# More pairs with seven products, and operand sums kept in DRAM, in the down projections of a two-layer decoder trunk

## The chip, the core and the metric

The kernel runs on one core of one Trainium2 chip. The metric is device time in microseconds (us). The engines are named as the profile names them: PE (TensorE, matrix products; PEld is its weight loads), DVE (VectorE), ACT (ScalarE), POOL (GpSimd) and SP (SyncE). Each engine executes its own instructions in the order in which the build has put them, and waits on semaphores for the others. Here SP does nothing but issue DMAs, and POOL little else.

## The reference

The model has two layers over 256 tokens of width 2048, all in float32: a gated linear attention layer and a block-sparse attention layer, each followed by the same channel mixer. The change lies in the two channel mixers (a convolutional SwiGLU with 5632 hidden features):

```python
def conv_ffn(x, norm_w, w_up, conv_w, conv_b, w_down):
    S = x.shape[1]
    h = rms_norm(x, norm_w) @ w_up
    hp = jnp.pad(h, ((0, 0), (CONV_WIDTH - 1, 0), (0, 0)))
    acc = conv_b
    for j in range(CONV_WIDTH):
        acc = acc + conv_w[j] * hp[:, j:j + S]
    a, u = jnp.split(acc, 2, axis=-1)
    return (jax.nn.silu(a) * u) @ w_down
```

```python
    for layer in range(DEPTH):
        if layer < N_A_LAYERS:
            h = h + gla_mixer(...)
        else:
            ...
            h = h + moba_mixer(...)
        h = h + conv_ffn(h, ffn_norm[layer], ffn_w_up[layer], ffn_conv_w[layer],
                         ffn_conv_b[layer], ffn_w_down[layer])
    return h
```

## The kernel before

**Products and their parts.** Every operand of a matrix product is kept as a high part (a cast to fp32r) and a low part (the remainder), and a product is high times high, low times high and high times low. `split` (L371) does this for activations; for weights ACT makes `whi` (L127) and DVE makes `wlo` (L128).

**The weight stream.** `WeightStream` brings all weights in chunks of 128 x 2048 floats (1 MB), in the order in which they are used, on SP's queue. A chunk lands in one of four `raw` buffers (`wraw`), and each half of 1024 columns is split into a `whi` and a `wlo`: three halves out of four into one of three `parts` buffers, the fourth into two slots of the pool `big`. `step` hands out one half; `prefetch` keeps the splits two to three halves ahead and the loads four chunks ahead (six in the down projections). A buffer of `raw` is free again when the second `wlo` made from it is done. `big` has 35 slots of 4 KB a partition, which also hold hidden activations, sums and residuals.

**Up projections.** There are 44 groups in each layer, two steps for one half of them each: `gemm` (L325) does 16 matmuls of 512 columns with `whi` (L332) and 16 of 256 with `wlo` (L334) in two steps. Then `ffn` (L634) makes the hidden activations (`hid`, 22 tiles, one for each pair of k-tiles below). During these stages `make_ahead` (L301) also prepares weight sums for the down projections: it loads a chunk of `w_dn` into a `raw` buffer (L308), adds in place with four DVE operations (L306, L307), and stores 1 MB to DRAM (`tsum`, L311, POOL's queue). The jobs are due at fixed counts of steps: the first after 24 and then every 12 for layer 0, the first after 8 and then every 12 for layer 1.

**Down projections.** `down` (L664) computes the 2048 output features in two blocks of 1024. A block goes over 22 pairs of k-tiles in an order that `ORDERS` writes out. An ordinary pair is a 2 x 2 block product with eight products of three matmuls each (L694). A pair with a `+` or `^` uses the seven products of the Strassen-Winograd scheme: 21 matmuls, with four sums of the activations and four sums of the weights. The weight sums come back from `tsum`, for `+` into a `raw` buffer and for `^` into two slots (`sums`). The sums of the activations (`combine`, L605, tile names `comb` and `whole`) are made in the up projections for the pairs in `EARLY`, and otherwise in the down projections by `combine_parts` (L629), at places 1, 3, 5, ... of a block. Of every four pairs with sums, three get a slot of their own, and the fourth uses what the three leave free. After the last pair with seven products, `u_sums` (L729) adds the products up; the last up to three ordinary pairs of a block (`_tail`) then run in two halves, and each half is closed with further additions (L776 for the last layer). The next block needs the PSUM banks that these additions free.

The order of instructions on each engine is decided by the framework's scheduler on a timeline of its own; the semaphores between engines follow from the tiles.

Of the kernel before, what the change touches and what calls it, by code (L numbers as in the profile page):

```python
# [18 lines left out]
S = 256  # L19
# [18 lines left out]
def _order(text):  # L38


    return [(int(k.rstrip("+^")), k[len(k.rstrip("+^")):]) for k in text.split()]


EARLY = (1, 3, 5, 7)
ORDERS = [[_order("0 1+ 2 3^ 4 5+ 6 7^ 8 9+ 11^ 10 13+ 15^ 12 16+ 17^ 14 19+ 18 20 21"),
           _order("0 2 4 6 1+ 3^ 8 5+ 7^ 10 9+ 11^ 12 13+ 15^ 14 16+ 17^ 18 19+ 20 21")],
          [_order("0 1+ 2 3^ 4 5+ 6 7^ 8 9+ 11^ 10 13+ 15^ 12 16+ 17^ 14 19+ 18 20 21"),
           _order("0 1+ 2 3+ 5^ 4 7+ 9^ 6 11+ 13^ 8 15^ 16+ 10 17^ 19^ 18 12^ 14^ 20 21")]]


def _tail(order):
# [89 lines left out]
def trunk(ctx: ExitStack, tc: tile.TileContext, xT, cst, msk, w1p, w2a, w_k, w_qa, w_v2, w_v, w_g, w_go,  # L141
# [2 lines left out]
    V, A, T = nc.vector, nc.scalar, nc.tensor  # L144

    keep = ctx.enter_context(tc.tile_pool(name="keep", bufs=1))
    big = ctx.enter_context(tc.tile_pool(name="big", bufs=35))
    raw = ctx.enter_context(tc.tile_pool(name="raw", bufs=4))
    parts = ctx.enter_context(tc.tile_pool(name="parts", bufs=3))
    tmp = ctx.enter_context(tc.tile_pool(name="tmp", bufs=6))  # L150
# [5 lines left out]
    def slot(shape, dt, name):  # L156
        return big.tile(shape, dt, name=name, tag="slot")
# [143 lines left out]
    def make_ahead(layer, w, first, every):  # L301

        def work(at):
            t = raw.tile([128, 2048], F32, name="wraw")
            b12, b11, b22, b21 = (t[:, 512 * i:512 * i + 512] for i in range(4))
            jobs = [lambda: V.tensor_sub(b22, b22, b12), lambda: V.tensor_sub(b12, b12, b11),  # L306
                    lambda: V.tensor_add(b11, b22, b11), lambda: V.tensor_sub(b21, b21, b11)]  # L307
            nc.sync.dma_start(t, ws.rows(w, at[0], 2048 * at[1]))  # L308
            for i, job in enumerate(jobs):
                after(4 + i, job)  # L310
            after(8, lambda: nc.gpsimd.dma_start(parked[layer][at], t))  # L311

        for i, at in enumerate(ahead[layer]):
            after(first + every * i, lambda at=at: work(at))
# [56 lines left out]
    def split(dst_hi, dst_lo, src):  # L371
        A.copy(dst_hi, src)
        V.tensor_sub(dst_lo, src, dst_hi.bitcast(F32))
# [19 lines left out]
                self.col = column_rstd(self.acc)  # L393


    make_ahead(0, w_dn0, 24, 12)
    nrm = Norm(C_GN, "xw", columns=True)
    for p in range(2):
        nrm.operand(p)
# [202 lines left out]
        for n in norms:  # L602
            after(2, n.close)

    def combine(k, hid_k, halves_):  # L605

        (a0, a1), (b0, b1) = halves_
        t = temp("comb", (128, 4, 128))
        V.tensor_add(t[:, 0], a1, b1)
        V.tensor_sub(t[:, 1], t[:, 0], a0)  # L610
        V.tensor_sub(t[:, 2], a0, a1)
        V.tensor_sub(t[:, 3], b0, t[:, 1])
        n = len(combos)
        if n % 4 < 3:
            rooms.append(slot([128, 4, 2, 128], F32R, "comb"))
            c = rooms[-1]
            split(c[:, 0:3, 0], c[:, 0:3, 1], t[:, 0:3])
            combos[k] = [(c[:, f, 0], c[:, f, 1]) for f in range(3)]
        else:
            combos[k] = [(c[:, 3, 0], c[:, 3, 1]) for c in rooms[-3:]]  # L620
            for f, parts_ in enumerate(combos[k]):
                split(*parts_, t[:, f])
        combos[k].append((hid_k[:, 0, 128:S], hid_k[:, 0, S + 128:]))
        split(*combos[k][3], t[:, 3])

    rooms = []
    combos = {}

    def combine_parts(k, hid):  # L629
        t = temp("whole")  # L630
        V.tensor_add(t, hid[k][:, :, :S], hid[k][:, :, S:])
        combine(k, hid[k], [(t[:, i, :128], t[:, i, 128:]) for i in range(2)])

    def ffn(layer, nrm, then):  # L634
        xs = rows(nrm.xs)
        hid = []
        combos.clear()
        whole = [None, None]
        cw = C_CW + layer * 3 * 2 * FT
        cb = C_CB + layer * 2 * FT  # L640
        for j in range(FT):
            ps = gemm(xs, KT)
            t = both(ps, "up")
            V.tensor_mul(t, t, bc(nrm.rstd))  # L644
            au = temp("au")
            for i in range(2):
                n = i * FT + j
                A.activation(au[:, i, :], t[:, i, :], AF.Identity, bias=col(cb + n),  # L648
                             scale=col(cw + 2 * 2 * FT + n))
                V.scalar_tensor_tensor(au[:, i, 1:], t[:, i, :S - 1], col(cw + 2 * FT + n), au[:, i, 1:],  # L650
                                       op0=OP.mult, op1=OP.add)
                V.scalar_tensor_tensor(au[:, i, 2:], t[:, i, :S - 2], col(cw + n), au[:, i, 2:],  # L652
                                       op0=OP.mult, op1=OP.add)
            A.activation(au[:, 0, :], au[:, 0, :], AF.Silu)
            V.tensor_mul(au[:, 0, :], au[:, 0, :], au[:, 1, :])
            if j % 2 == 0:
                hid.append(slot([128, 2, 2 * S], F32R, "hid"))
            split(hid[-1][:, j % 2, :S], hid[-1][:, j % 2, S:], au[:, 0, :])
            whole[j % 2] = (au[:, 0, :128], au[:, 0, 128:])
            if j % 2 and j // 2 in EARLY:  # L660
                combine(j // 2, hid[-1], whole)
        then(hid)

    def down(layer, hid, ready, jobs):  # L664

        def late(k):
            return lambda: combine_parts(k, hid)

        done = set(EARLY)
        for b, order in enumerate(ORDERS[layer]):  # L670
            new = [k for k, seven in order if seven and k not in done]
            done |= set(new)
            todo = dict(jobs.get(b, {}))
            for i, k in enumerate(new):
                todo.setdefault(1 + 2 * i, []).append(late(k))
            low = acc_ps.tile([128, 2, 512], F32, name="acc")
            p = {2: low[:, 0], 3: low[:, 1], 4: bank("p4", (128, 512)), 8: bank("p8", (128, 512))}
            left = dict.fromkeys(range(1, 9), 0)
            for k, seven in order:
                for n in ((1, 5, 7, 6, 4, 3, 2) if seven else (2, 3, 4, 8, 2, 3, 4, 8)):  # L680
                    left[n] += 3
            begun = set()

            def prods(*todo):

                w = step()
                for n, _, _ in todo:
                    if n not in p:
                        two = acc_ps.tile([128, 2, 512], F32, name="acc")
                        p.update({n: two[:, 0], {1: 6, 5: 7}[n]: two[:, 1]})  # L690
                for xi, wi in ((0, 0), (1, 0), (0, 1)):
                    for n, x, f in todo:
                        left[n] -= 1
                        T.matmul(p[n], x[xi], w[wi][:, 512 * f:512 * f + 512], start=n not in begun, stop=left[n] == 0)  # L694
                        begun.add(n)

            def part(k, i, t):
                x = hid[k][:, i, 128 * t:]
                return x[:, :128], x[:, S:S + 128]

            def comb(k, f):
                return combos[k][f]

            last = max(i for i, (k, seven) in enumerate(order) if seven)
            tail = [k for k, _ in order[len(order) - _tail(order):]]
            for i, (k, seven) in enumerate(order[:len(order) - len(tail)]):
                for job in todo.get(i, ()):
                    job()
                if seven:
                    prods((1, part(k, 0, 0), 0))  # L710
                    prods((3, comb(k, 3), 0), (2, part(k, 1, 0), 1))
                    prods((6, comb(k, 1), 1), (5, comb(k, 0), 0))
                    prods((7, comb(k, 2), 0), (4, part(k, 1, 1), 1))
                else:
                    for a in range(2):
                        prods(*((n, part(k, a, t), f)
                                for n, t, f in ((2, 0, a), (3, 0, 1 - a), (4, 1, a), (8, 1, 1 - a))))
                if i == last:
                    sums = ready(b, p)
            for f, (n0, n1) in enumerate(((2, 4), (3, 8))):  # L720
                for i, k in enumerate(tail):
                    for job in todo.get((f, i), ()):
                        job()
                    prods(*((n, part(k, a, t), a) for a in range(2) for n, t in ((n0, 0), (n1, 1))))
                if f:
                    ws.prefetch(cur[0])
                sums(f, (n0, n1))
# [217 lines left out]
        ox.append(o)  # L945

    xkv = []
    make_ahead(1, w_dn1, 8, 12)
    after(12, bias_rows)
    for p in range(NP):  # L950
        after(26 + p, lambda p=p: xkv.append(make_xw(p, C_KVN, "xkv")))
# [148 lines left out]
```

## Time and profile before

| | us |
|---|---|
| median of 3 runs (2212.78 to 2212.98) | 2212.93 |
| the profiled execution | 2212.01 |
| its span | 2210.2 |
| DVE busy | 1731.5 |
| ACT busy | 1292.6 |
| up projections of layer 0, some | 412 to 877 |
| its down blocks | 877 to 989, 989 to 1105 |
| up projections of layer 1, some | 1505 to 1982 |
| its down blocks | 1983 to 2095, 2095 to 2206 |

The stages in the lower rows are times from the start of the span. In the profile's rows, `out<-in` names the tile written and the tiles read, without buffer numbers; `xN` counts instructions; after the bar stand the busy time, the mean time of one in ns, and the idle time of the engine just before them with what ended it. `SPq` and `POOLq` are the queues on which SP and POOL issue DMAs; the figure at the end of such a row is the median time from issue to landing. In the windows each engine has its busy time and, in brackets, its instructions; then come the granted clock of PE as a share of full speed, the mean share of the 16 DMA engines, and GB/s.

### The profile page before, as it was taken

How to read it: one execution, taken by the hardware profiler on the slowest of the kernel's cores; microseconds unless marked ns; L12 is line 12 of the kernel's file. 1: busy time of each engine (PE TensorE's matmuls, PEld its weight loads, DVE VectorE, ACT ScalarE, POOL GpSimd, SP SyncE). 2: the span in 40 equal slices, each digit the busy share in tenths (PEclk: the TensorE clock that was granted, in tenths of full speed). 3: DMA queues.
4: the chain of work that ended last, by engine and by line, in shares of the span. 5: the costliest groups of instructions: out<-in, count | busy, mean ns of one | idle time of the engine just before them, and what ended most of it. 6: DMA issues, size and time to landing. Idle time of an engine off the chain costs nothing.

```text
span 2210.2 us, 30840 instructions
## 1 busy us (share of the span) xinstructions
PE 2203.1 (100%) x11742; PEld 1902.4 (86%) x11742; DVE 1731.5 (78%) x2478; ACT 1292.6 (58%) x1825; POOL 69.5 (3%) x107
## 2 busy tenths in 40 slices
PE   9999999999999999999999999999999999999999
PEld 7889888888888888888888888888888888888887
DVE  6676877788888887977777676678888888788876
ACT  6655644665555555656556665546665555556564
POOL 0000000000000000000010000000000000000000
PEclk9999999999999999999999999999999999999999
DMA  7675577676677775788867665676777676768895
GB/s 299 214 253 201 208 271 270 244 272 249 240 265 247 248 266 201 277 288 293 303 213 265 246 243 195 218 265 251 259 265 248 247 266 234 261 238 293 285 364 192
DMA packets 86631, 561.20 MB, mean 254 GB/s; under 512 B 10145, under 2 KB 10673, under 8 KB 27602
## 3 DMA queue, kind: packets, MB, share of 16 engines
q1 hardware_dynamic: 76050, 499.85, 63.8%
q0 software_dynamic: 9856, 58.80, 6.8%
q8 instruction: 92, 1.51, 0.3%
q10 hardware_dynamic: 576, 0.58, 0.1%
q14 instruction: 57, 0.47, 0.1%
HBM read 504.64 MB, written 54.55 MB: 253 GB/s over the span
## 4 chain that ended last, share of the span: by engine, by line
PE 98%; DMA 1%; DVE 1%; ACT 0%; issue 0%; SPq 0%; ACTq 0%; DVEq 0%
PE acc L332 40%; PE acc L334 21%; PE acc L694 13%; PE acc L347 10%; PE p L694 6%; PE acc L350 5%; PE sT L538 0%; DVE wlo L128 0%; DMA wraw<-w_v 0%; PE tr L891 0%; ACT whi L127 0%; PE s L909 0%; DMA wraw<-w_dn 0%; PE pT L929 0%; PE z L444 0%; PE oT L424 0%
## 5 line engine op out<-in xcount | busy, mean ns | idle before, releaser
L127 ACT CAST whi<-wraw 128x1024 fp32r<-128x1024 f32 (+1 forms) x832 | 839.5, 1024 | 604.9 <-PE acc L332 319.1
L128 DVE TENSOR_TENSOR wlo<-wraw,whi 128x1024 fp32r<-128x1024 f32 (+1 forms) x832 | 973.0, 1188 | 273.7 <-ACT whi L127 155.3
L332 PE MATMUL acc<-xw,whi 128*128 128x512 f32 x3328 | 796.9, 391 | 0.0
L332 PEld LDWEIGHTS acc<-xw,whi 128*128 128x128 f32 x3328 | 610.8, 188 | 117.9
L334 PEld LDWEIGHTS acc<-xw,wlo 128*128 128x128 f32 x3328 | 426.8, 191 | 16.1
L334 PE MATMUL acc<-xw,wlo 128*128 128x256 f32 x3328 | 432.6, 283 | 0.0
L694 PE MATMUL acc<-whi,hid 128*128 128x512 f32 x612 | 183.5, 390 | 0.0
L694 PE MATMUL p<-whi,hid 128*128 128x512 f32 x428 | 139.4, 389 | 0.0
L694 PEld LDWEIGHTS acc<-whi,hid 128*128 128x128 f32 x612 | 114.6, 188 | 23.6
L347 PE MATMUL acc<-whi,xkv 128*128 128x512 f32 x512 | 134.5, 394 | 0.0
L347 PE MATMUL acc<-whi,xw 128*128 128x512 f32 x512 | 129.0, 392 | 1.6 <-ACT whi L127 1.6
L650 DVE SCALAR_TENSOR_TENSOR au<-up,cs,au 128x255 f32<-128x255 f32 x176 | 83.0, 481 | 48.0 <-ACT au L648 47.7
L347 PEld LDWEIGHTS acc<-whi,xw 128*128 128x128 f32 x512 | 95.3, 188 | 22.5 <-ACT whi L127 2.5
L347 PEld LDWEIGHTS acc<-whi,xkv 128*128 128x128 f32 x512 | 93.7, 188 | 17.8
L360 ACT COPY up<-acc 128x512 f32<-128x512 f32 x88 | 51.5, 585 | 88.9 <-PE acc L334 88.8
L694 PE MATMUL acc<-wlo,hid 128*128 128x512 f32 x306 | 100.1, 390 | 0.3 <-DVE wlo L128 0.3
L648 ACT ACTIVATE au<-up,cs 128x256 f32<-128x256 f32 x176 | 96.1, 593 | 6.5 <-DVE up L644 5.8
L694 PEld LDWEIGHTS p<-whi,hid 128*128 128x128 f32 x428 | 80.3, 188 | 16.8
L694 PE MATMUL acc<-whi,comb 128*128 128x512 f32 x276 | 83.0, 389 | 0.0
L652 DVE SCALAR_TENSOR_TENSOR au<-up,cs,au 128x254 f32<-128x254 f32 x176 | 80.9, 476 | 0.0
L694 PE MATMUL p<-wlo,hid 128*128 128x512 f32 x214 | 70.9, 389 | 0.0
L350 PE MATMUL acc<-wlo,xkv 128*128 128x512 f32 x256 | 69.8, 391 | 0.0
(261 smaller groups left out, 2076.7 us busy)
## 6 DMA issues: line engine op xcount, KB each, us to landing
wraw<-w_up SPq DMA_DIRECT2D x176, 1024.0 KB, 6.1
wraw<-w_dn SPq DMA_DIRECT2D x88, 1024.0 KB, 4.9
tsum<-wraw POOLq DMA_DIRECT2D x46, 1024.0 KB, 6.4
wraw<-w_dn SPq DMA_DIRECT2D x46, 768.0 KB, 5.9
wraw<-tsum SPq DMA_DIRECT2D x23, 1024.0 KB, 6.6
sums<-tsum SPq DMA_DIRECT2D x46, 512.0 KB, 6.9
wraw<-w_g SPq DMA_DIRECT2D x16, 1024.0 KB, 5.5
wraw<-w_go SPq DMA_DIRECT2D x16, 1024.0 KB, 5.2
```

The source lines that it names most:

```text
L127: nc.scalar.copy(hi[:, a:b], src[:, a:b])
L128: nc.vector.tensor_sub(lo[:, a:b], src[:, a:b], hi[:, a:b].bitcast(F32))
L332: T.matmul(ps[:, b, :], two[i][0][:, c:c + 128], xs(kt), start=kt == 0, stop=False)
L334: T.matmul(ps[:, b, :S], two[i][1][:, c:c + 128], xs(kt)[:, :S], start=False, stop=kt == kts - 1)
L347: T.matmul(ps[:, t, :], xs(kt)[:, x0 + 128 * t:x0 + 128 * t + 128], hi[:, c:c + 512], start=kt == 0 and x0 == 0, stop=False)
L350: T.matmul(ps[:, t, :], xs(kt)[:, 128 * t:128 * t + 128], lo[:, c:c + 512], start=False, stop=kt == KT - 1)
L360: A.copy(t, ps[:, :, S:])
L648: A.activation(au[:, i, :], t[:, i, :], AF.Identity, bias=col(cb + n), scale=col(cw + 2 * 2 * FT + n))
L650: V.scalar_tensor_tensor(au[:, i, 1:], t[:, i, :S - 1], col(cw + 2 * FT + n), au[:, i, 1:], op0=OP.mult, op1=OP.add)
L652: V.scalar_tensor_tensor(au[:, i, 2:], t[:, i, :S - 2], col(cw + n), au[:, i, 2:], op0=OP.mult, op1=OP.add)
L694: T.matmul(p[n], x[xi], w[wi][:, 512 * f:512 * f + 512], start=n not in begun, stop=left[n] == 0)
```

## The change

The number of pairs with seven products goes from 46 to 53: 11 to 13 in the first block of each layer, 11 to 12 in the second block of layer 0, and 13 to 15 in the second block of layer 1. The orders change with it; the halved tail of the first blocks is two pairs instead of three. For the pairs in `ASIDE` the four activation sums are made in the up projections, three of them split into a slot and written to DRAM (`aside`, 384 KB, POOL's queue), and brought back into their room by a DMA on POOL's queue in the first block of the down projections, where they were made before. The sums still made late in a first block are those of pairs 17, 19, 12 and 14; the sums of 10 and 8 are made in the last block of layer 1. The jobs of a block now stand at its places 0, 1, 2, ... instead of 1, 3, 5, .... A pair that the last block doesn't use as a seven (`kept` False) has its fourth sum in its room and not in `hid`. `make_ahead` prepares 25 chunks instead of 22 for layer 0 (every 11 steps instead of 12) and 28 instead of 24 for layer 1 (from step 6 every 10 instead of from step 8 every 12). `big` gets a 36th slot, and the buffer for software DMA descriptors is halved.

```diff
--- before.py
+++ after.py
@@ -41,11 +41,13 @@
     return [(int(k.rstrip("+^")), k[len(k.rstrip("+^")):]) for k in text.split()]
 
 
+
 EARLY = (1, 3, 5, 7)
-ORDERS = [[_order("0 1+ 2 3^ 4 5+ 6 7^ 8 9+ 11^ 10 13+ 15^ 12 16+ 17^ 14 19+ 18 20 21"),
-           _order("0 2 4 6 1+ 3^ 8 5+ 7^ 10 9+ 11^ 12 13+ 15^ 14 16+ 17^ 18 19+ 20 21")],
-          [_order("0 1+ 2 3^ 4 5+ 6 7^ 8 9+ 11^ 10 13+ 15^ 12 16+ 17^ 14 19+ 18 20 21"),
-           _order("0 1+ 2 3+ 5^ 4 7+ 9^ 6 11+ 13^ 8 15^ 16+ 10 17^ 19^ 18 12^ 14^ 20 21")]]
+ASIDE = (9, 11, 13, 15, 16)
+MADE = (9, 11, 13, 17, 15, 16, 19, 12, 14, 10, 8)
+FIRST = "0 1+ 2 3^ 5+ 4 7^ 9+ 6 11^ 13+ 8 15^ 16+ 10 17^ 19+ 18 12^ 14+ 20 21"
+ORDERS = [[_order(FIRST), _order("0 2 4 6 1+ 3^ 8 5+ 7^ 10 9+ 11^ 18 13+ 15^ 14 16+ 17^ 19+ 12^ 20 21")],
+          [_order(FIRST), _order("0 1+ 3^ 2 5+ 7^ 9+ 4 11^ 13+ 15^ 6 16+ 17^ 19+ 18 12^ 14^ 10^ 8^ 20 21")]]
 
 
 def _tail(order):
@@ -144,7 +146,7 @@
     V, A, T = nc.vector, nc.scalar, nc.tensor
 
     keep = ctx.enter_context(tc.tile_pool(name="keep", bufs=1))
-    big = ctx.enter_context(tc.tile_pool(name="big", bufs=35))
+    big = ctx.enter_context(tc.tile_pool(name="big", bufs=36))
     raw = ctx.enter_context(tc.tile_pool(name="raw", bufs=4))
     parts = ctx.enter_context(tc.tile_pool(name="parts", bufs=3))
     tmp = ctx.enter_context(tc.tile_pool(name="tmp", bufs=6))
@@ -393,7 +395,7 @@
                 self.col = column_rstd(self.acc)
 
 
-    make_ahead(0, w_dn0, 24, 12)
+    make_ahead(0, w_dn0, 24, 11)
     nrm = Norm(C_GN, "xw", columns=True)
     for p in range(2):
         nrm.operand(p)
@@ -602,34 +604,60 @@
         for n in norms:
             after(2, n.close)
 
-    def combine(k, hid_k, halves_):
-
+    combos = {}
+    rooms = []
+    aside = dram.tile([2, len(ASIDE), 128, 768], F32R, name="aside")
+
+    def room(k, hid_k, kept):
+
+
+        n = len(combos)
+        if n % 4 < 3:
+            rooms.append(slot([128, 4, 2, 128], F32R, "comb"))
+            combos[k] = [(rooms[-1][:, f, 0], rooms[-1][:, f, 1]) for f in range(3)]
+        else:
+            combos[k] = [(c[:, 3, 0], c[:, 3, 1]) for c in rooms[-3:]]
+        combos[k].append((hid_k[:, 0, 128:S], hid_k[:, 0, S + 128:]) if kept else
+                         (rooms[-1][:, 3, 0], rooms[-1][:, 3, 1]))
+        return rooms[-1] if n % 4 < 3 else None
+
+    def sums(halves_):
         (a0, a1), (b0, b1) = halves_
         t = temp("comb", (128, 4, 128))
         V.tensor_add(t[:, 0], a1, b1)
         V.tensor_sub(t[:, 1], t[:, 0], a0)
         V.tensor_sub(t[:, 2], a0, a1)
         V.tensor_sub(t[:, 3], b0, t[:, 1])
-        n = len(combos)
-        if n % 4 < 3:
-            rooms.append(slot([128, 4, 2, 128], F32R, "comb"))
-            c = rooms[-1]
-            split(c[:, 0:3, 0], c[:, 0:3, 1], t[:, 0:3])
-            combos[k] = [(c[:, f, 0], c[:, f, 1]) for f in range(3)]
+        return t
+
+    def combine(k, hid_k, halves_, kept=True):
+
+        t = sums(halves_)
+        own = room(k, hid_k, kept)
+        if own is not None and not kept:
+            return split(own[:, :, 0], own[:, :, 1], t)
+        if own is not None:
+            split(own[:, 0:3, 0], own[:, 0:3, 1], t[:, 0:3])
         else:
-            combos[k] = [(c[:, 3, 0], c[:, 3, 1]) for c in rooms[-3:]]
-            for f, parts_ in enumerate(combos[k]):
-                split(*parts_, t[:, f])
-        combos[k].append((hid_k[:, 0, 128:S], hid_k[:, 0, S + 128:]))
+            for f in range(3):
+                split(*combos[k][f], t[:, f])
         split(*combos[k][3], t[:, 3])
 
-    rooms = []
-    combos = {}
-
-    def combine_parts(k, hid):
+    def put_aside(layer, k, hid_k, halves_):
+        t = sums(halves_)
+        c = slot([128, 3, 2, 128], F32R, "aside")
+        split(c[:, :, 0], c[:, :, 1], t[:, 0:3])
+        nc.gpsimd.dma_start(aside[layer, ASIDE.index(k)], c.rearrange("a b c d -> a (b c d)"))
+        split(hid_k[:, 0, 128:S], hid_k[:, 0, S + 128:], t[:, 3])
+
+    def take_back(layer, k, hid_k):
+        own = room(k, hid_k, True)
+        nc.gpsimd.dma_start(own[:, 0:3].rearrange("a b c d -> a (b c d)"), aside[layer, ASIDE.index(k)])
+
+    def combine_parts(k, hid, kept):
         t = temp("whole")
         V.tensor_add(t, hid[k][:, :, :S], hid[k][:, :, S:])
-        combine(k, hid[k], [(t[:, i, :128], t[:, i, 128:]) for i in range(2)])
+        combine(k, hid[k], [(t[:, i, :128], t[:, i, 128:]) for i in range(2)], kept)
 
     def ffn(layer, nrm, then):
         xs = rows(nrm.xs)
@@ -659,20 +687,24 @@
             whole[j % 2] = (au[:, 0, :128], au[:, 0, 128:])
             if j % 2 and j // 2 in EARLY:
                 combine(j // 2, hid[-1], whole)
+            if j % 2 and j // 2 in ASIDE:
+                put_aside(layer, j // 2, hid[-1], whole)
         then(hid)
 
     def down(layer, hid, ready, jobs):
 
-        def late(k):
-            return lambda: combine_parts(k, hid)
-
+        sevens = [{k for k, seven in order if seven} for order in ORDERS[layer]]
         done = set(EARLY)
         for b, order in enumerate(ORDERS[layer]):
             new = [k for k, seven in order if seven and k not in done]
             done |= set(new)
             todo = dict(jobs.get(b, {}))
+            new.sort(key=MADE.index)
             for i, k in enumerate(new):
-                todo.setdefault(1 + 2 * i, []).append(late(k))
+                kept = k in sevens[-1]
+                todo.setdefault(i, []).append(
+                    (lambda k=k: take_back(layer, k, hid[k])) if k in ASIDE else
+                    (lambda k=k, kept=kept: combine_parts(k, hid, kept)))
             low = acc_ps.tile([128, 2, 512], F32, name="acc")
             p = {2: low[:, 0], 3: low[:, 1], 4: bank("p4", (128, 512)), 8: bank("p8", (128, 512))}
             left = dict.fromkeys(range(1, 9), 0)
@@ -945,7 +977,7 @@
         ox.append(o)
 
     xkv = []
-    make_ahead(1, w_dn1, 8, 12)
+    make_ahead(1, w_dn1, 6, 10)
     after(12, bias_rows)
     for p in range(NP):
         after(26 + p, lambda p=p: xkv.append(make_xw(p, C_KVN, "xkv")))
@@ -1088,7 +1120,7 @@
         "rel": np.ascontiguousarray(a["rel_bias"]),
         "onehot": _buckets(),
     }
-    nc = bacc.Bacc("TRN2", target_bir_lowering=False, num_devices=1, dynamic_dma_scratch_size=4096)
+    nc = bacc.Bacc("TRN2", target_bir_lowering=False, num_devices=1, dynamic_dma_scratch_size=2048)
     args = [nc.dram_tensor(n, v.shape, mybir.dt.from_np(v.dtype), kind="ExternalInput").ap()
             for n, v in arrays.items()]
     args.append(nc.dram_tensor("out_0_dram", (2, 128, D), F32, kind="ExternalOutput").ap())
```

## The prediction

> **What bounds the kernel now.** I read the page's busy times and chain of waits first, then the windows by stage, then the chain inside the few places where the matrix engine (PE) is not busy.
>
> ```profile
> span 2210.2 us, 30840 instructions
> PE 2203.1 (100%) x11742; PEld 1902.4 (86%) x11742; DVE 1731.5 (78%) x2478; ACT 1292.6 (58%) x1825; POOL 69.5 (3%) x107
> PE 98%; DMA 1%; DVE 1%; ACT 0%; issue 0%; SPq 0%; ACTq 0%; DVEq 0%
> ```
>
> PE is busy for 2203.1 of 2210.2 us and carries 98% of the chain, so a matmul taken out is worth its pace, and any lateness elsewhere costs only where PE runs dry. The windows tell how near to that each stage is (columns: window, total, PE, PEld, DVE, ACT, POOL, granted clock, DMA share, GB/s).
>
> ```profile
> 412.00:876.00 464.00, 464.00 (x2671) 410.13 (x2671) 388.58 (x586) 273.34 (x393) 6.93 (x13) 1.00 0.70 248
> 877.00:989.00 112.00, 111.83 (x494) 92.26 (x493) 92.26 (x130) 68.85 (x87) 1.45 (x3) 1.00 0.80 286
> 989.00:1105.00 116.00, 116.00 (x521) 96.11 (x520) 84.46 (x90) 69.46 (x81) 2.82 (x6) 1.00 0.81 295
> 1505.00:1982.00 477.00, 477.00 (x2756) 421.77 (x2755) 397.48 (x596) 284.14 (x410) 11.26 (x21) 1.00 0.71 253
> 1983.00:2095.00 112.00, 111.83 (x494) 92.26 (x493) 96.03 (x142) 70.53 (x92) 2.18 (x4) 1.00 0.83 292
> 2095.00:2206.00 111.00, 111.00 (x492) 91.87 (x490) 82.56 (x89) 62.81 (x70) 2.14 (x4) 1.00 0.77 285
> ```
>
> In order these are layer 0's up projections, its two down blocks, layer 1's up projections and its two down blocks. PE loses time only in the first down block of each layer, 0.18 us each. The chain there shows why:
>
> ```profile
> 908.70 1.15 DVE wlo L128
> 909.85 0.04 issue
> 909.89 0.73 PE acc L694 x2
> 910.63 0.46 PE p L694 x2
> ...
> 1073.01 4.99 PE acc L694 x22
> ```
>
> A wlo on DVE ends last; the two matmuls behind it take 0.73 us, the next two 0.46. DVE had no free moment around it:
>
> ```profile
> 897.00:907.00 10.00, 10.00 (x46) 8.29 (x45) 10.00 (x20) 7.08 (x12) 0.00 (x0) 1.00 0.57 204
> 907.00:917.00 10.00, 9.82 (x43) 7.82 (x43) 10.00 (x22) 6.50 (x9) 0.00 (x0) 1.00 0.94 335
> 2013.00:2023.00 10.00, 9.82 (x43) 7.82 (x43) 10.00 (x22) 6.51 (x9) 1.10 (x2) 1.00 0.93 324
> ```
>
> **The saving.** A run of 22 down matmuls takes 4.99 us, 0.227 each. An ordinary pair has 24 (5.45 us), a pair with seven products 21 (4.77 us). Seven pairs more (two in each first block, one in layer 0's second, two in layer 1's second) take out 21 matmuls: 21 x 0.227 = 4.77 us.
>
> **The entry to the down stages.** Operand sums made late cost DVE in the stage where it is full.
>
> ```profile
> L128 DVE TENSOR_TENSOR wlo<-wraw,whi 128x512 fp32r<-128x512 f32 x23 | 15.7, 684 | 1.1 <-issue 1.1
> ...
> L631 DVE TENSOR_TENSOR whole<-hid 128x512 f32<-128x512 f32 x9 | 6.2, 685 | 1.2 <-DMA out_dram<-res 1.2
> ...
> L610 DVE TENSOR_TENSOR comb<-comb,whole 128x128 f32<-128x128 f32 x9 | 2.6, 285 | 0.0
> ...
> L373 DVE TENSOR_TENSOR comb<-comb 128x384 fp32r<-128x384 f32 x7 | 3.9, 552 | 0.0
> ...
> L373 DVE TENSOR_TENSOR hid<-comb,hid 128x128 fp32r<-128x128 f32 x9 | 2.6, 286 | 0.0
> ```
>
> One late sum is 0.685 + 4 x 0.285 + 0.552 + 0.286 = 2.66 us of DVE. The first blocks drop from seven to four of them, 8.0 us less; two pairs more with seven products bring back little (a seven's wlo is one of 512 and three of 1024 columns, 0.68 + 3 x 1.22 = 4.34 us of DVE, an ordinary pair's two are 2.44, so +3.8 us). DVE is ahead by 4.2 us net, and the stall should go: each is 0.18 + (0.73 - 0.46) = 0.45 us, two make -0.90 us. If it stays, the term is 0; if a stall of the same kind comes elsewhere as well, +0.90.
>
> **What the up projections take on.** Each of five pairs per layer adds four adds and a split there, 4 x 0.285 + 0.552 + 0.286 = 1.98 us of DVE, and a store; layer 0 makes three weight pairs more, layer 1 four, each of four DVE operations:
>
> ```profile
> L306 DVE TENSOR_TENSOR wraw<-wraw 128x512 f32<-128x512 f32 x26 | 17.8, 685 | 1.8 <-DMA wraw<-w_dn 1.8
> L307 DVE TENSOR_TENSOR wraw<-wraw 128x512 f32<-128x512 f32 x26 | 17.8, 683 | 0.0
> L128 DVE TENSOR_TENSOR wlo<-wraw,whi 128x1024 fp32r<-128x1024 f32 x171 | 206.1, 1220 | 32.8 <-PE acc L334 24.7 <-ACT whi L127 6.5 <-issue 1.5
> L127 ACT CAST whi<-wraw 128x1024 fp32r<-128x1024 f32 x170 | 176.4, 1049 | 106.9 <-PE acc L332 91.5 <-DMA wraw<-w_up 10.9 <-issue 4.5
> ```
>
> For layer 1 that is 4 x 2.74 + 5 x 1.98 = 20.9 us on 397.5 of 477: DVE at 88%, covered by its idle time as a sum. What isn't covered is the time at which buffers come free. A weight pair being made holds one of the four load buffers from its load until its store has landed, and the next load into that buffer waits for the store.
>
> ```profile
> SPq L104 <- DVE wlo L128: 230.3, 49, 10.7
> SPq L104 <- DVE au L655: 140.2, 22, 7.7
> SPq L104 <- DMA tsum<-wraw: 30.4, 12, 3.8
> ```
>
> ```profile
> wraw<-w_up SPq DMA_DIRECT2D x81, 1024.0 KB, 6.1
> tsum<-wraw POOLq DMA_DIRECT2D x13, 1024.0 KB, 7.6
> ```
>
> ```profile
> 1602.38 1.91 PE acc L334 x16
> 1604.29 3.65 PE acc L332 x16
> ```
>
> SP already waits for that store 12 times, 2.5 us each, with every weight load of the stage queued behind it. Two steps are 3.65 + 1.91 = 5.56 us of PE, so one pair made every 12 steps had 33.4 us, and every 10 steps has 27.8. A load needs, after the wlo that frees its buffer has been placed, 1.22 + 6.1 + 1.05 = 8.4 us until its whi is there (wlo, landing, cast); after a store 7.6 + 6.1 + 1.05 = 14.75 us. I counted in the instruction orders of both kernels how much PE work (0.227 us for a matmul of 512 columns, 0.12 = 1.91 / 16 for 256) lies between the place of the freeing instruction and the first matmul on the load. Before, in the body of layer 1's up projections, 9 us more than needed is the least. After, eight loads are short: by 1.75 (behind a store), twice 1.9 and five times 0.4, together 7.6 us. Layer 0, at every 11, is never short.
>
> Bounds: a shortfall counted from the load's own place in SP's order (at most 4.0, eleven places) adds to 26 us. But before has loads in the down stages that by this second count are short by 1.7 (twice), and PE didn't wait for them; taking 1.7 off each leaves 10.3. And if DVE runs ahead of the places by 2 us, nothing remains: the lower end is 0. I take 6.5, a little under the first count, which is nearest to what the earlier orders bear out (places with 0 to 0.5 to spare that cost nothing). The unhidden cost is the wait at the head of SP's queue; ACT's cast is next late, and in its order stand the casts for the halves behind.
>
> **Layer 1, from block to block.** Two late sums (pairs 10 and 8, 2 x 2.66 = 5.3 us) fall on the first two places of the last block, instead of the first and third, among the additions that close the finished block, and the first seven's 4.34 us of wlo.
>
> ```profile
> 2085.00:2095.00 10.00, 10.00 (x46) 8.29 (x45) 8.84 (x17) 3.88 (x8) 0.00 (x0) 1.00 0.69 203
> 2095.00:2105.00 10.00, 10.00 (x46) 8.29 (x45) 8.63 (x15) 6.02 (x8) 2.14 (x4) 1.00 0.77 247
> ```
>
> DVE had 1.16 and 1.37 us free here. One more sum in this window is 2.66: between 0 (order absorbs it) and 2.66 late; what lies between, 2.66 - 1.37 = 1.3 us, I take. The make-loads' POOL traffic at this place is not on that path.
>
> **The last blocks' transfers.** A seven moves 768 + 1024 KB, 1.835 MB, in 4.77 us, 385 GB/s; three or four of these in a row now occur.
>
> ```profile
> 2100.00:2182.00 82.00, 82.00 (x364) 67.89 (x363) 60.06 (x59) 51.51 (x57) 0.82 (x2) 1.00 0.94 350
> 2110.00:2120.00 10.00, 10.00 (x46) 8.29 (x45) 7.10 (x7) 6.94 (x8) 0.00 (x0) 1.00 1.02 415
> 2130.00:2140.00 10.00, 10.00 (x45) 8.26 (x44) 6.51 (x7) 6.62 (x7) 0.00 (x0) 1.00 1.01 397
> ```
>
> The rate 415 was reached with all queues full, and 350 / 0.94 = 372 is what the mean makes of a full share. The last block's 15 sevens and 7 ordinary pairs move 34.9 MB, 1.57 more than before. Lower end 0 (at 385 or more nothing queues), upper end 1.57 MB / 0.35 MB per us = 4.5 us. By the same count of places, two loads in the chains are short, 1.3 (layer 0) and 0.2 (layer 1). I take 1.0. The Trainium skill (DMA: Bandwidth & Descriptors, Bandwidth) gives some 358 GB/s as the limit of one core's HBM transfers; by it the chains would queue and the term would be about 4.4 instead of 1.0. The trace's 415 and 397 over 10 us disagree with it as a hard limit.
>
> A 36th slot, the smaller descriptor ring and the ten aside writes and reads (384 KB on POOL's queue, 3% busy) I cost at nothing: POOL's idle time hides their issue; if the reads land late, a seven in the first block waits, up to the 6.9 us that a parked half takes here:
>
> ```profile
> sums<-tsum SPq DMA_DIRECT2D x46, 512.0 KB, 6.9
> ```
>
> Sum: -4.77 - 0.90 + 6.5 + 1.3 + 1.0 = +3.1 us. The profiled execution (2212.01, 1.8 of it around the span) becomes 2215.1; the median of the runs is 0.92 above it, so **2216 us**.
>
> **Rivals.** *The saving stays whole* (chance 0.28): DVE and SP run ahead of their places, as before's orders show it for the down stages, where several dozen casts stand 0.2 to 0.9 us ahead of their matmul, less than their 1.05 us, and PE lost 0.90 us in all. For it: no up stage waits today. Against: no up order of before came near its needs. 2212.93 - 4.77 - 0.90 = 2207.3; faster, if less than 1.3 us is given back. *The load buffers of layer 1's up projections starve outright* (0.20): loads go at SP's own places, 26 us instead of 6.5, 2235; with the 1.7 taken off each, 10.3, 2220. It decides from about 8 us on. For it: eleven places at a period of 27.8 us; against: shortfalls of 1.7 by this count were harmless in the down stages. *The transfers bind in the last block alone* (0.07, and by the quoted page's rule more): -5.67 + 4.5 = -1.2, 2211.7, no change. *The change doesn't do what it says* (0.03), the stages being ruled by DVE so that fewer matmuls only raise PE's waiting: 2213.
>
> **How the numbers follow.** A measurement here can tell 0.2%, 4.4 us, from no change. My forecast (0.42) reaches from 2211 to 2220, 0.25 of it within 0.2% and 0.17 above 2217.4. Faster 0.28 from the first rival; within 0.25 + 0.07 + 0.03 = 0.35; slower 0.17 + 0.20 = 0.37. Range: 2206.5 (whole saving and a little more) to 2226 (half-way into starvation), some 2 in 10 outside.
>
> **What would show it.** The down matmuls count 1953 instead of 1974 and PE has no gap near 910 and 2015. In layer 1's up projections the PE waits for a cast, itself behind a load of w_up, at some eight places, most of them 22 to 44 us apart, summing to 6.5 us; layer 0's have none. PE waits about 1.3 us for a wlo at the head of the last block. The forecast is wrong if the up projections show no wait, or one of over 10 us, or if a take-back is what a first block waits for.

## The result, and the profile after

| | before | changed |
|---|---|---|
| median, us (6 runs each) | 2213.01 (2212.78 to 2214.01) | 2226.26 (2225.02 to 2227.02) |
| ratio, 95% interval | | 1.0057 (1.0046 to 1.0068) |
| profiled execution, us | 2212.01 | 2225.02 |
| its span, us | 2210.2 | 2223.2 |

The changed kernel is slower by 13.25 us, 0.6%. That lies 0.26 us above the upper end of the predicted range (2206.5 to 2226) and four times as far from before as the point of 2216 (+3.1), on the same side.

The page of the changed kernel (section 1, then the chain's shares by engine from section 4):

```profile
PE 2203.9 (99%) x11721; PEld 1897.7 (85%) x11721; DVE 1762.8 (79%) x2539; ACT 1302.6 (59%) x1848; POOL 85.9 (4%) x134
PE 95%; DMA 2%; DVE 1%; ACT 1%; issue 1%; SPq 0%; DVEq 0%; ACTq 0%
```

The 21 matmuls are gone (11742 before, 11721 now), but PE is no longer the whole chain: 95% instead of 98%. The windows of the same stages in the changed kernel (window, total, PE, PEld, DVE, ACT, POOL, granted clock, DMA share, GB/s) show where it runs dry:

```profile
412.00:876.00 464.00, 464.00 (x2670) 410.13 (x2669) 399.80 (x624) 276.75 (x403) 11.72 (x22) 1.00 0.72 262
877.00:988.00 111.00, 110.84 (x488) 90.99 (x487) 89.88 (x115) 69.73 (x85) 3.57 (x7) 1.00 0.87 320
988.00:1103.00 115.00, 114.18 (x510) 93.73 (x509) 84.82 (x90) 67.17 (x80) 2.14 (x4) 1.00 0.78 293
1503.00:1995.00 492.00, 480.13 (x2751) 420.19 (x2750) 406.94 (x632) 280.22 (x415) 16.05 (x30) 1.00 0.69 254
1995.00:2108.00 113.00, 112.90 (x506) 93.46 (x505) 94.53 (x123) 72.77 (x91) 3.75 (x7) 1.00 0.90 329
2108.00:2220.00 112.00, 111.47 (x492) 91.97 (x490) 90.45 (x102) 67.72 (x77) 2.13 (x4) 1.00 0.78 296
```

Layer 1's up projections lose 11.87 us of PE, layer 0's none. The down blocks lose 0.16, 0.82 and 0.10; the last window reaches beyond the last matmul, so its 0.53 is the end of the kernel. DVE in the up projections is at 406.94 of 492, 83%: it is not the bound. PE's waits in that stage, from the view of waits:

```profile
PE acc L334 <- ACT whi L129: 11.9, 12, 1.4
```

Twelve waits, all for a cast: nine of 1.13 to 1.36 us, 10.4 us together, and three of 0.30 to 0.70. One of the nine in the chain of waits (start, length, what):

```profile
1676.06 1.85 PE acc L334 x8
1677.91 0.02 issue
1677.94 1.05 ACT whi L129
1678.99 0.04 issue
1679.03 3.01 PE acc L334 x12
```

and the same place in the timeline (in brackets the idle time before and what ended it):

```profile
1675.90 2.00 PE L334 MATMUL acc<-xw,whi 128*128 128x512 f32 x8
...
1677.94 1.04 ACT L129 CAST whi<-wraw 128x1024 fp32r<-128x1024 f32 x1 [1.25 <-PE acc L334]
...
1679.03 2.33 PE L334 MATMUL acc<-xw,whi 128*128 128x512 f32 x9 [1.13 <-ACT whi L129]
```

I had predicted a cast that waits for a load; this one does not. ACT sat idle for 1.25 us until PE finished the eight matmuls directly ahead, then cast, then PE could go on. The two engines take turns where they should overlap. The semaphores of the built order say the same: this `whi` goes into the `parts` buffer that those eight matmuls are reading. I counted such casts, whose buffer is freed by the matmuls just ahead of their own user: none in the order of the kernel before, ten in the changed one, all in layer 1's up projections, and nine of those with no matmul between. The nine long waits of the trace stand at the places of these nine, and the wait of 0.70 us at that of the tenth. At the other two, of 0.30 and 0.44 us, the cast stood on ACT behind an instruction that waited for DVE. A load delayed only one of the twelve: the cast at 1629.81, by 0.2 us.

### The profile page after: what moved, and what is told of

It reads as the page before. It is cut to its first block, busy times and chain, and to the rows that moved or that the text cites. A ratio compares the mean times of both kernels' runs of the same rounds, so it can differ in the third digit from the quotient of the medians.

```text
span 2223.2 us, 31020 instructions
## 1 busy us (share of the span) xinstructions
PE 2203.9 (99%) x11721; PEld 1897.7 (85%) x11721; DVE 1762.8 (79%) x2539; ACT 1302.6 (59%) x1848; POOL 85.9 (4%) x134
## 4 chain that ended last, share of the span: by engine, by line
PE 95%; DMA 2%; DVE 1%; ACT 1%; issue 1%; SPq 0%; DVEq 0%; ACTq 0%
PE acc L334 38%; PE acc L336 20%; PE acc L726 13%; PE acc L349 10%; PE p L726 5%; PE acc L352 5%; ACT whi L129 1%; DMA wraw<-w_dn 1%; DVE wlo L130 1%; DMA wraw<-w_up 0%; DMA sums<-tsum 0%; PE sT L540 0%; DMA wraw<-tsum 0%; DMA wraw<-w_v 0%; PE tr L923 0%
## 5 line engine op out<-in xcount | busy, mean ns | idle before, releaser
L334 PE MATMUL acc<-xw,whi 128*128 128x512 f32 x3328 | 801.7, 392 | 11.9 <-ACT whi L129 11.9
L726 PE MATMUL acc<-whi,hid 128*128 128x512 f32 x596 | 175.1, 390 | 0.6 <-ACT whi L129 0.5
L726 PE MATMUL p<-whi,hid 128*128 128x512 f32 x386 | 124.6, 390 | 0.0
L726 PE MATMUL acc<-whi,comb 128*128 128x512 f32 x320 | 96.2, 390 | 0.1
L308 DVE TENSOR_TENSOR wraw<-wraw 128x512 f32<-128x512 f32 x106 | 73.0, 688 | 27.0 <-DMA wraw<-w_dn 26.1
L130 DVE TENSOR_TENSOR wlo<-sums,whi 128x1024 fp32r<-128x1024 f32 x54 | 65.8, 1224 | 27.1 <-ACT whi L129 22.3
L726 PEld LDWEIGHTS p<-whi,hid 128*128 128x128 f32 x386 | 72.4, 188 | 15.1
L129 ACT CAST whi<-sums 128x1024 fp32r<-128x1024 f32 x54 | 56.5, 1053 | 43.2 <-PE p L726 25.3
```

What stands on the lines that cost most here:

```text
L129: nc.scalar.copy(hi[:, a:b], src[:, a:b])
L130: nc.vector.tensor_sub(lo[:, a:b], src[:, a:b], hi[:, a:b].bitcast(F32))
L334: T.matmul(ps[:, b, :], two[i][0][:, c:c + 128], xs(kt), start=kt == 0, stop=False)
```

## The experiments

**First question: what put those casts there.** The prediction's cause was the period of ten steps, which would starve the load buffers. The rival came from `prefetch`: every fourth half goes to two slots instead of a `parts` buffer, by the running count `n % 4 == 3`. A pair with seven products has four halves, an ordinary one two. Three pairs more in layer 0 shift the count by 6. Layer 1's up projections began at half 564, a multiple of 4, and begin now at 570; the half that goes to slots was the fourth of each group's four steps and is now the second.

*phase*: the changed kernel, with the slot half put back.

```diff
-            if deep and n % 4 == 3:
+            if deep and (n + (2 if n >= 442 else 0)) % 4 == 3:
```

> The changed kernel, with one thing altered: from half 442 on (the first after layer 0's down projections) the half that goes to slots is the one with (n+2) mod 4 = 3 instead of n mod 4 = 3. The change added 3 pairs with seven products in layer 0, each with 4 halves instead of 2, so the count of halves is shifted by 6 and the slot half of each up projection of layer 1 became the second of its four steps instead of the fourth. Theory A (the shift makes the waits: the built order then holds ten casts that reuse the buffer of the matmuls directly before them): all waits of 1.3 us in layer 1's up projections go, PE idle there falls from 11.9 to below 1 us, time 2226.3 - 14 to 16 = 2210 to 2212. Rival B (the period of ten steps starves the load buffers, as predicted): the loads come as before, time stays within 2 us of 2226.

Measured: 2211.15 us (11 runs), 0.9991 of before (0.9982 to 0.9999), 15.1 us below the changed kernel. The window of layer 1's up projections:

```profile
1503.00:1980.00 477.00, 477.00 (x2755) 421.75 (x2754) 405.93 (x633) 286.38 (x419) 15.51 (x29) 1.00 0.73 263
```

PE is never idle there, with the period still at ten steps and five pairs still put aside. Theory A's number holds, the rival's does not. The stage is 15 us shorter than in the changed kernel (477 against 492).

*before_shifted*: the kernel before, with only its slot half moved.

```diff
-            if deep and n % 4 == 3:
+            if deep and (n + (2 if n >= 436 else 0)) % 4 == 3:
```

> The kernel before, with the slot half of layer 1 (from half 436 on) moved by two: no pair, sum or period is changed. Theory A: the waits of 1.3 us come up in the kernel before as well, about seven of them (so many casts in the built order reuse the buffer of the matmuls directly before them), 2213 + 7 x 1.3 + 1 = about 2223. Rival B: nothing of it touches the load buffers' period, 2213 within 1 us.

Measured: 2224.5 us, 1.0052 (1.0037 to 1.0068). The waits of PE in layer 1's up projections, and one of them in the chain:

```profile
PE acc L332 <- ACT whi L127: 9.7, 8, 1.8
```

```profile
1651.98 1.85 PE acc L332 x8
1653.84 0.02 issue
1653.86 1.05 ACT whi L127
1654.91 0.04 issue
1654.96 3.92 PE acc L332 x16
```

The pattern is that of the changed kernel to the hundredth, without any part of the described change. Seven of the eight waits are of this kind, as many as I had counted; the eighth, 1.77 us at the start of the stage, is not. The last row has a second cost: 16 matmuls after a wait take 3.92 us instead of 3.65.

*before_every10* and *after_every12* exchange the periods.

```diff
-    make_ahead(1, w_dn1, 8, 12)
+    make_ahead(1, w_dn1, 8, 10)
```

> The kernel before, with layer 1's 24 weight pairs made every 10 steps instead of every 12. Theory A: no wait in the up projections, 2213 within 1.5 us. Rival B (my prediction's step): waits of PE of 5 to 10 us in layer 1's up projections, 2218 to 2223.

Measured: 2213.0 us, 0.9999 (0.999 to 1.0008). The load buffers stand a period of ten steps without a loss; the trace has no wait of PE in layer 1's up projections.

```diff
-    make_ahead(1, w_dn1, 6, 10)
+    make_ahead(1, w_dn1, 6, 12)
```

> The changed kernel, with layer 1's weight pairs made every 12 steps instead of every 10 (the last of the 28 then fall into the down projections). Theory A: the built order still has five to six such casts, so 5 x 1.3 = 6 to 7 us of waits stay in layer 1's up projections: about 2218 to 2221, plus what the last pairs cost in the down blocks. Rival B: the waits go altogether, 2212 or less.

Measured: 2233.15 us, 1.009 (1.0076 to 1.0104), slower than the changed kernel; the expected 2218 to 2221 was missed. The waits in the up projections stay, as theory A has it: PE 477.80 of 487, ten waits of 9.2 us in all. Six of them are such casts (five of 1.13 us and one of 0.70, 6.4 us, as counted); at the other four the cast follows, on ACT, an instruction of another kind. And I had given the late pairs no price. In the down block the chain shows it:

```profile
1503.00:1990.00 487.00, 477.80 (x2743) 419.32 (x2742) 402.23 (x622) 278.28 (x412) 15.50 (x29) 1.00 0.69 251
...
2040.00:2048.00 8.00, 3.64 (x9) 2.87 (x10) 4.75 (x6) 3.46 (x4) 0.54 (x1) 0.61 0.86 346
```

```profile
2021.62 9.97 DMA tsum<-wraw
2031.59 0.02 issue
2031.61 11.58 DMA wraw<-w_dn
...
2043.26 1.05 ACT whi L129
```

Here it is the predicted mechanism: a load that waits for a made pair's store, 9.97 + 11.58 us, and PE dry at its end. It exists, but in the down block, where loads have less time (a pair with seven products needs 1.8 MB in 4.77 us, the up projections 1 MB in 5.56 us).

**Second question: is it the buffer, or the place of the slot half as such?**

*even_sevens*: the changed kernel with one seven less in layer 0, so that the count is a multiple of four again. The stream's code is untouched. In this kernel the fourth sum of pair 12 shares its place with another of its sums in layer 0's first block, so that block's output is not the reference's.

```diff
-ORDERS = [[_order(FIRST), _order("0 2 4 6 1+ 3^ 8 5+ 7^ 10 9+ 11^ 18 13+ 15^ 14 16+ 17^ 19+ 12^ 20 21")],
+ORDERS = [[_order(FIRST), _order("0 2 4 6 1+ 3^ 8 5+ 7^ 10 9+ 11^ 18 13+ 15^ 14 16+ 17^ 19+ 12 20 21")],
```

> The changed kernel with pair 12 of layer 0's second block as an ordinary pair (52 pairs with seven products, 24 of them in layer 0 instead of 25); the weight stream is as in the changed kernel. The halves counted before layer 1 are then a multiple of four again. Theory A (the slot half's place decides): no wait of 1.3 us in layer 1's up projections, time as with the slot half moved, 2211, plus 3 matmuls (0.7) and less what the four sevens in a row cost at the end of layer 0 (up to 1.2): 2210.5 to 2212. Rival (the added work of layer 1 or the amount of pairs makes the waits): 2225 or more.

Measured: 2211.55 us, 0.9994 (0.9985 to 1.0003). The trace has no wait of PE in layer 1's up projections: the count of layer 0's sevens alone takes them away.

*shifted_4parts*: the slow variant of the kernel before, with a fourth `parts` buffer.

```diff
-            if deep and n % 4 == 3:
+            if deep and (n + (2 if n >= 436 else 0)) % 4 == 3:
-    big = ctx.enter_context(tc.tile_pool(name="big", bufs=35))
+    big = ctx.enter_context(tc.tile_pool(name="big", bufs=34))
-    parts = ctx.enter_context(tc.tile_pool(name="parts", bufs=3))
-    tmp = ctx.enter_context(tc.tile_pool(name="tmp", bufs=6))
+    parts = ctx.enter_context(tc.tile_pool(name="parts", bufs=4))
+    tmp = ctx.enter_context(tc.tile_pool(name="tmp", bufs=5))
```

> The run before_shifted (the kernel before with the slot half of layer 1 moved to the second of four steps, 2224.5) with four parts buffers instead of three; to make room, 34 slots instead of 35 and 5 temporaries instead of 6. Theory A in its narrow form (the wait is a cast that must take the parts buffer which the matmuls just ahead of its own user are still reading): with a fourth buffer the built order holds no such cast in the up projections, the seven waits of 1.3 us go, 2213 to 2215 (the smaller pools may cost a little in the down blocks). Rival (the place of the slot half slows the stage in another way, by loads or by DVE): 2222 or more.

Measured: 2219.5 us, 1.0031 (1.002 to 1.0042); the expected 2213 to 2215 was missed. The waits of PE in layer 1's up projections:

```profile
PE acc L332 <- ACT whi L127: 1.9, 1, 1.9
```

The seven repeated waits are gone, with the slot half where it was; so they hung on the buffer. The one at the start of the stage stays (1.77 us in before_shifted, 1.93 here), so that one didn't. The total is 5.0 us below before_shifted, not the 10 expected. Part of the rest lies in the last layer's first down block, where PE waits 1.0 us for wlo; the smaller pools may be its reason, which no run separates.

*slot_first_step*: the changed kernel with the slot half at another step. It is the first of the four steps, as the label has it; the expectation's word "third" is a slip of mine.

```diff
-            if deep and n % 4 == 3:
+            if deep and (n + (1 if n >= 442 else 0)) % 4 == 3:
```

> The changed kernel, with the slot half of layer 1 moved so that it is the third of the four steps of an up projection ((n+1) mod 4 = 3), instead of the second (as changed) or the fourth (the run phase). The built order holds no cast tied to the matmuls just ahead. Theory A: no waits of 1.3 us, 2211 within 1.5. Rival (only the fourth step is harmless, since its half ends a group): waits as in the changed kernel, 2220 or more.

Measured: 2251.69 us, 1.0177 (1.016 to 1.0194). Theory A missed by 40 us: no cast is tied to the matmuls just ahead, and PE waits all the same. From the waits of PE, and from the chain before the second longest (3.79 us):

```profile
PE acc L334 <- ACT whi L129: 27.5, 22, 4.7
```

```profile
1640.88 7.39 DMA wraw<-w_dn
...
1651.26 0.60 DVE wraw L309
1651.86 0.21 DVE comb L628
1652.08 0.02 issue
1652.10 0.51 ACT comb L374
1652.61 0.96 ACT whi L129
1653.57 0.04 issue
1653.61 2.50 PE acc L334 x5
```

Read backwards: PE waits for a cast that stands on ACT behind the cast of a sum (`comb`), which waits for DVE, which stands behind the additions of a weight pair, which waited for that pair's load. The slot half's place decides the order in which the scheduler puts the casts; the tie to a buffer is one way in which a bad order costs, a cast queued last of all on ACT another. The waits alone don't make the 40 us: in the stage's window (1505 to 2028) PE is also busy for 494.58 us, 18 more than in phase, at a granted clock of 0.97 (see the last section).

**Third question: the other terms of the sum.** All three runs keep the slot half moved back.

*phase_no_aside*: no pair is put aside; nine sums are made late in each first block.

```diff
-ASIDE = (9, 11, 13, 15, 16)
+ASIDE = ()
-            if deep and n % 4 == 3:
+            if deep and (n + (2 if n >= 442 else 0)) % 4 == 3:
```

> The changed kernel with the slot half moved in layer 1 (as in the run named phase, 2211.2) and with no pair set aside: the sums of 9, 11, 13, 15 and 16 are made late, at the first places of the first blocks, nine late sums there instead of four. My prediction's price is 2.66 us of DVE for each, 5 x 2.66 = 13.3 us more in a stage in which DVE has little to spare: waits of PE of 2 to 8 us for wlo in each first block, 2215 to 2225. Rival (the late sums cost nothing that PE waits for): 2211 within 1.

Measured: 2216.06 us, 1.0017 (1.0008 to 1.0026), 4.9 us above phase (5.3 if each is taken against its own runs of before): the putting aside earns that much, at no cost in the up projections that PE sees. The time is in the expected range, the waits are smaller than expected: about 1.4 us in the window of each first block instead of 2 to 8, and half of that for casts, not for wlo.

*spread_a* and *spread_b*: ordinary pairs put between the sevens at the entries and at the end of layer 0. The orders of spread_a (those of spread_b begin their first blocks differently):

```diff
-FIRST = "0 1+ 2 3^ 5+ 4 7^ 9+ 6 11^ 13+ 8 15^ 16+ 10 17^ 19+ 18 12^ 14+ 20 21"
+FIRST = "0 1+ 2 3^ 4 5+ 7^ 6 9+ 11^ 8 13+ 15^ 10 16+ 17^ 19+ 18 12^ 14+ 20 21"
-ORDERS = [[_order(FIRST), _order("0 2 4 6 1+ 3^ 8 5+ 7^ 10 9+ 11^ 18 13+ 15^ 14 16+ 17^ 19+ 12^ 20 21")],
+ORDERS = [[_order(FIRST), _order("0 2 4 1+ 3^ 6 5+ 7^ 8 9+ 11^ 10 13+ 15^ 14 16+ 17^ 18 19+ 12^ 20 21")],
```

> The slot half moved in layer 1 (as in phase), and orders that put ordinary pairs between: the first blocks begin 0 1+ 2 3^ 4 5+ 7^ 6 (before's beginning) instead of 0 1+ 2 3^ 5+ 4 7^ 9+, and the second block of layer 0 ends 16+ 17^ 18 19+ 12^ 20 21 instead of four sevens in a row. The waits for casts behind sums<-tsum at the entries (0.79 + 0.18 and 1.07 + 0.19) and the two at the end of layer 0 (0.72 + 0.45) are what is left above the saving: if each goes, 2211.2 - 3.4 = 2207.8. If they only move, 2210 to 2212.

> As spread_a, but the first blocks begin 0 2 1+ 4 3^ 5+ 6 7^ 9+ 8: ordinary pairs earlier still, so that the first parked sums are needed one pair later. If the entry's wait is the landing of sums<-tsum, it goes: 2207.8 as in spread_a. If it is DVE that is behind (late sums on the first places), it stays at some 0.9 in all: 2208.5 to 2210.

Measured: 2211.42 (0.9991, 0.9982 to 1.0000) and 2211.13 (0.9991, 0.9982 to 1.0000): neither differs from phase. The waits only moved; for spread_b that was neither of the two outcomes that I had named (2207.8, or 2208.5 to 2210). Its wait at the entry of layer 0 is gone, but 0.9 us of waits for wlo come later in each first block, and 0.9 us for casts in layer 1's. In spread_a the second block of layer 0 is better (114.76 of 115), but the entry of the first is worse (109.38 of 111, against 110.36 in phase), its cast again behind parked sums:

```profile
877.00:988.00 111.00, 109.38 (x485) 89.98 (x485) 90.20 (x115) 69.69 (x85) 2.64 (x5) 1.00 0.88 316
988.00:1103.00 115.00, 114.76 (x514) 94.33 (x513) 84.81 (x91) 67.79 (x80) 3.24 (x7) 1.00 0.82 301
```

## Why the prediction came out as it did

**The saving** was right: 21 matmuls, 4.77 us. Once the waits of layer 1 are out, phase shows what is left of it: 2.2 us below its own runs of before (2211.15 against 2213.36, with an interval that ends just below 1).

**The entry stalls** (-0.90): wrong in the net. The old ones at 909 and 2015 are gone, as DVE's lead was to give. Others came at 885 and 889, and in layer 1 at 2024. The first of them is a cast behind one that waited for parked sums, in the chain of the changed kernel

```profile
874.28 8.65 DMA sums<-tsum
...
885.00 0.95 ACT whi L129
885.96 0.04 issue
886.00 0.50 PE acc L726
```

These sums are issued when they were before (at 873.8 us, before at 873.6) and land about 1 us later: the longest landing there is 8.7 us instead of 7.8, with three of the take-backs, which I had cost at nothing, issued at 871.75 to 876.83. But what makes PE wait is the place of their cast in ACT's order, in the timeline of before and then of the changed kernel:

```profile
886.77 1.05 ACT L127 CAST whi<-sums 128x1024 fp32r<-128x1024 f32 x1
882.96 1.05 ACT L129 CAST whi<-sums 128x1024 fp32r<-128x1024 f32 x1 [3.01 <-DMA sums<-tsum]
```

Before, ACT first did the activations of the last up group and the casts needed next, and by then the sums had landed. Now these stand behind the cast of the sums, and ACT sits idle for 3.01 us. In phase and spread_a the order is the same and ACT waits there for 3.52 and 4.50 us; in spread_b and phase_no_aside the cast comes later (at 894.38 and 888.99) and waits for no landing, and PE has no wait at 885. I had looked at DVE alone.

**What the up projections take on** (+6.5): this is the step that failed. The place was right, layer 1's up projections and not layer 0's, and so was the sign, but the mechanism was the wrong one and the size less than half. I wrote that what isn't covered "is the time at which buffers come free", and meant the four load buffers, at a period of ten steps. before_every10 shows that a period of ten steps costs nothing (2213.0), and phase that the loads of the changed kernel come in time. The buffers that came free too late are the three of `parts`, by the place of the slot half. The twelve waits are 11.9 us, ten of them, 11.1 us, such casts; each wait also slows the matmuls behind it, by 3.92 - 3.65 = 0.27 us for sixteen, 3.2 us for the twelve waits. Together that is 15.1 us; the stage's window is 15 us longer than in phase, and phase as a whole is 15.1 us faster (2226.26 - 2211.15).

That the forecast named the right stage and came so near to its range is therefore luck: the count that led there was of loads, and it is the count `n % 4`, which the prediction nowhere mentions, that made the waits. The rival in which the load buffers starve outright had the measured time between its two prices (2220 and 2235), and by the same runs it is out as well.

Behind it stands my reading of the order. I had seen casts 0.2 us ahead of their matmul and set them aside, since the down stages of before held several dozen of these and lost 0.90 us in all. Those were free to go earlier than their place. The ones in layer 1's up projections were not: each waited for the matmuls directly in front. I looked at how late a cast stood and not at what it waited for.

**From block to block in layer 1** (+1.3): nothing was seen; the window from 2104 to 2114 has PE at 10.00 and DVE at 9.08.

**The last blocks' transfers** (+1.0): close in size, but only in part by the transfers. In the chain of the changed kernel one wait, at 1066 us, ends on a load that took 9.38 us, and another, at 1090, on a wlo. Both lie at the end of layer 0 and cost 0.82 us of idle PE together, 0.52 of it behind the load; layer 1's chains of three and four sevens show none. In the last block PE is busy for all of the 80.00 us from 2120 to 2200, while 365 GB/s are moved. The rival that the transfers bind in the last block is out.

**The sum**, with what was measured for each term: -4.77 - 0.90 + 15.1 + 0.82 + 0.16 + 0.10 (the idle time of the down blocks' windows) = 10.5. Of the 13.0 us between the two profiled executions 2.5 are left. The matmuls behind the five waits in the down blocks, at 0.27 us each, are 1.35 of it; the rest has no name.

## What to carry to other kernels

A counter that runs through the whole program (here `n % 4`) couples stages that seem to have nothing to do with each other: three pairs more in one layer moved a buffer choice in the next, and that cost three times what the whole change saved (15.1 against 4.77 us). After a change of counts, compare each later stage's order with the old one even if the diff doesn't touch it.

When an order is read before a run, ask of each late instruction what it waits for. A cast placed just ahead of its user is harmless if it may run earlier, and costs its whole length if its buffer is held by the instruction in front. A cast placed early can cost as well: if it waits for a landing, as that of the parked sums did, all that stands behind it on its engine waits too.

## What the runs showed of the hardware that was not expected

After a wait of 2 us PE's granted clock fell. In slot_first_step a wait of 2.06 us is followed by 16 matmuls in 5.56 us instead of 3.65; the chain, and the windows around it:

```profile
1745.68 1.92 PE acc L336 x16
...
1749.64 5.56 PE acc L334 x16
1755.20 1.91 PE acc L336 x16
```

```profile
1747.00:1751.00 4.00, 1.95 (x11) 1.50 (x11) 4.00 (x8) 2.34 (x5) 0.00 (x0) 0.99 0.24 68
1751.00:1755.00 4.00, 4.00 (x12) 3.13 (x11) 3.33 (x7) 1.09 (x2) 0.53 (x1) 0.58 0.89 320
1755.00:1760.00 5.00, 5.00 (x31) 4.43 (x30) 2.20 (x4) 2.56 (x4) 0.00 (x0) 1.00 1.03 400
```

The clock is 0.58 in the mean of the 4 us from 1751 to 1755 (0.50 from 1751 to 1754) and then full again: this wait of 2.06 us cost 2.06 + 5.56 - 3.65 = 4.0 us. In after_every12 it is 0.61 in the mean of the window around the wait behind the 11.58 us load. The Trainium skill (TensorE: Matmul & The Clock Gate, HAM oscillation) speaks of idle gaps above some 3.4 us; here one of 2.06 us was enough, though this was seen once only. A wait of 1.93 us in shifted_4parts left the clock at 1.00 in the windows from 1517 to 1530. Behind the waits of up to 1.36 us in the changed kernel the granted clock stays at 1.00 in the window of the stage, and the 0.27 us that the next sixteen matmuls lose there has no cause that these runs settle.
